# Staging the output gates by PSUM bank: from two shared tiles of 1024 columns to tiles of 512

## The chip, the cores and the metric

The kernel runs on one core of one Trainium2 chip. The metric is the device time of one execution in microseconds (us); lower is better. The kernel is written in Python with a tile framework. Its author gives the order of the program and the pools of buffers; a planner then lays out each engine's instruction stream by simulating the program with a cost table, taking what comes earlier in the program first where several instructions are ready. On the chip every engine works through its own stream in that order.

## What is computed

One layer of a trunk over 256 context tokens and 2048 latent tokens, 1024 wide:

```python
z = concat([hc, hx]) @ w_in                    # columns for four head groups
z_ml, z_rw, z_gl, z_gd = split(z)
mixed = concat([mlstm(z_ml), rwkv7(z_rw), gla(z_gl), gated_deltanet(z_gd)])
x = x + gate1 * (mixed[latent] @ w_out)
x = x + gate2 * (square(relu(rms(x) @ w1)) @ w2)
out = rms(x)
```

Each mixer runs a forward and a backward scan over 36 chunks of 64 tokens. The output of three of the mixers is multiplied by an **output gate**, a sigmoid or SiLU of columns of `z`: `sigmoid(o)` for mLSTM, `silu(og)` for GLA, `silu(zg)` for DeltaNet. The change concerns how these gates get from the product `z` to the place where the scans read them.

## The kernel before

**Stages.** The projection is computed in rounds over parts of the tokens. In each round the scans' inputs go to scratch tensors in HBM, and from there the scans take them chunk by chunk. After the fifth round comes a stage that the code calls the gap (L1889 and L1890): four calls of `out_gates`, each over 512 tokens, compute the output gates, and 16 scan steps (`group`) are interleaved with them, six forward (chunks 18 to 23) and ten backward (chunks 25 to 16). Then the tail follows: the output projection (`ps_o`), the MLP (`ps_f`, `ps_a`) and the last norm in four blocks of tokens, with the last 24 scan steps interleaved. The first tail block needs chunks 16 to 23 to be finished.

**An output gate tile.** `out_gates` (L1276) first builds the normed input `hh`, `hl` (`make_h`, L533: eight tiles `xh` of 512 columns are loaded, multiplied on GpSimd, scaled and copied on ScalarE and subtracted on VectorE; there is one `hh` and one `hl`, so the next `make_h` writes them when the last product has read them). Then it computes three gates through `gate_tiles` and `tm_tiles` (L861). `tm_pair` (L593) loads the weights, splits them in two parts (`w_hi`, `w_lo`) and multiplies: one PSUM bank `ps_z` takes 256 tokens by 256 columns, from 48 matmuls, and a tile of 512 tokens has two such banks. The pool `pd` has two banks in all. For each bank `fill` computes a tanh on ScalarE (into `gate`, a tile of the tag `b2`) and then, on VectorE, the gate itself into the staging tile, called `tm`. For a SiLU gate this last instruction reads the PSUM bank too. The staging tile is then stored to `x_gat` in HBM by `tm_out` (L636), which issues two DMAs per store on SyncE's queue (SP).

**Buffers.** The staging tile before is a `t4`: 1024 columns of the tag `x4`, of which there are two buffers (L1240). The tag `b2` has seven buffers of 512 columns (L1232). A buffer goes to its next tile when all readers and writers of the tile before it are done, a store's DMA included, and tiles take the buffers of a tag in the order of the program.

**Solves.** The RWKV and DeltaNet scans need triangular systems solved ahead of each pair of chunks (`solve`, L1287). A batch of up to four such units runs through three steps: `prep` per unit (loads, the products `ps_n`, a store to `x_sN`), one `find` for the batch (31 steps of two elementwise instructions, then a store to `x_sX`) and `post` per unit (loads, the products `ps_s` in two steps, a store to `x_t`). Each `prep`, `find` and `post` takes two tiles of 1024 columns. The batches queued in the fifth round (L1886) run beside each other: the first and third use the tags `s_b` and `s_x`, of one buffer each; the second, four units, uses **`x4`** for both tiles (L1847), the tag of the gates' staging tile. In the trace, which leaves buffer numbers out, the tiles on `x4` are called `s_x`, those on the other tags `s_s_b` and `s_s_x`.

**Order.** `interleave` takes one step of `out_gates` (one bank) at a time and then one entry of the solve queue. 24 steps remain of that queue when the gap begins: the last two `prep` of the second batch, the four `post` of the first, the second's `find`, the third's two `prep`, the second's four `post`, then the third's `find`, five empty entries, its two `post`, and three entries `ml_final`. So gate tiles and solve tiles alternate in the two buffers of `x4`. All of `ps_n`, `ps_s` and the scans' output products (`ps_ym`, `ps_ylgr`) share one PSUM buffer of the tag `yy`, in the order of the program.

Of the kernel before, what the change touches and what calls it, by code (L numbers as in the profile page):

```python
# [176 lines left out]
class Kern:  # L177
# [171 lines left out]
    def fill(self):  # L349

        X = self.X
        one = self.sp.tile([128, 1024], F32, tag="s_x", name="s_s_x", bufs=self.sb["s_x"])
        self.G.memset(one[:, :NCH], 1.0)
        for ft in range(2):
            c = 588 + 129 * ft
            for par, p in enumerate(SL):
                self.dma(X["tm"][:, :, par, c:c + 1].rearrange("c t o -> t c o"), one[p, :NCH].unsqueeze(2))
# [503 lines left out]
    def tm_tiles(self, i, chunks, dst, f0, fill, r=None):  # L861

        banks = self.tm_pair(i, r)
        st = self.t4("tm").rearrange("p (i r w) -> p i r w", r=2, w=128)
        for x, b in enumerate(banks):
            fill(st[:, 2 * x:2 * x + 2].rearrange("p i r w -> p i (r w)"), b)
            if x + 1 == len(banks) or chunks[x + 1] != chunks[x] + 4:
                a = next(j for j in range(x + 1) if chunks[x] - chunks[j] == 4 * (x - j))
                c0, n = chunks[a], 4 * (x + 1 - a)
                self.tm_out(st[:, 2 * a:2 * x + 2], dst[c0:c0 + n, :, :, f0:f0 + 128], n)  # L870
            yield
        if len(banks) == 1:
            yield
# [1054 lines left out]
```

## Time and profile before

| what | value |
| --- | --- |
| median of 3 runs | 4183.04 us (4180.95 to 4185.43) |
| the profiled execution | 4181.71 us |
| its span, from the first to the last instruction | 4179.9 us |
| mean granted TensorE clock | 0.875 |
| TensorE matmul busy | 3462.1 us (83%) |
| VectorE busy | 2490.3 us (60%) |
| ScalarE, GpSimd busy | 34%, 35% |

PE is TensorE's matmuls, PEld its weight loads, DVE is VectorE, ACT ScalarE, POOL GpSimd, SP SyncE, whose queue issues the DMAs. In rows of groups, a name such as `tm<-gate,ps_z` means that the instruction writes `tm` and reads `gate` and `ps_z`; `[4.76 <-DMA x_gat<-tm]` behind an instruction says that its engine sat idle for 4.76 us before it, and what ended that. Most elementwise instructions carry the line of a small helper (L185, L189, L193, L198), so tiles tell them apart.

### The profile page before, as it was taken

The numbers are of one execution on the slowest core, as the hardware profiler recorded it, in microseconds if no ns is written. First come the engines' busy times: TensorE is split into PE (matmuls) and PEld (weight loads), VectorE is DVE, ScalarE is ACT, GpSimd is POOL, SyncE is SP. The second block draws the span as 40 slices with busy tenths as digits, with TensorE's granted clock in tenths as the row PEclk, the third lists the DMA queues.
The fourth block names the chain that finished last, engine by engine and source line by source line (L and its number), as shares of the span: only waits on it lengthen the run. The fifth ranks groups of instructions, "written<-read, shape, count | busy, mean of one in ns | idle before, by whom it ended". The sixth has DMA issues, their size and how long they took to land.

```text
span 4179.9 us, 75082 instructions
## 1 busy us (share of the span) xinstructions
PE 3462.1 (83%) x29082; PEld 2807.3 (67%) x29082; DVE 2490.3 (60%) x5259; ACT 1403.3 (34%) x2544; POOL 1464.4 (35%) x1682
## 2 busy tenths in 40 slices
PE   6465877867777876658896999999999999999998
PEld 5344666656556765547785777777778777877786
DVE  6673866764776585536865556567754464445444
ACT  3334334434433433323332323233322332233222
POOL 3221834552626253502242333334322232223222
PEclk9667978877887876768898999999999999999999
DMA  5568478657686864647777444454532333232322
GB/s 205 108 180 149 116 157 194 143 131 146 153 150 160 187 144 124 171 121 193 212 212 195 124 135 148 138 171 142 175 95 96 106 102 115 96 98 91 104 96 86
DMA packets 610372, 592.66 MB, mean 142 GB/s; under 512 B 286384, under 2 KB 487168, under 8 KB 610016
## 3 DMA queue, kind: packets, MB, share of 16 engines
q1 hardware_dynamic: 610016, 587.87, 53.9%
q8 instruction: 229, 3.75, 0.4%
q14 instruction: 127, 1.04, 0.1%
HBM read 463.78 MB, written 123.92 MB: 141 GB/s over the span
## 4 chain that ended last, share of the span: by engine, by line
PE 42%; DVE 4%; issue 1%; POOL 1%; ACT 1%; DMA 1%; SPq 0%; POOLq 0%; DVEq 0%; ACTq 0%
PE ps_a L240 17%; PE ps_f L240 15%; PE ps_o L240 4%; PE ps_ylgr L229 1%; PE ps_z L212 1%; PE ps_S L229 1%; PE ps_att L240 1%; DVE h2l L193 1%; DVE relu L185 1%; PE ps_R L229 1%; SPq L201 0%; PE ps_ym L229 0%; PE ps_yT L248 0%; PE ps_ml L240 0%; POOL yall L185 0%
## 5 line engine op out<-in xcount | busy, mean ns | idle before, releaser
L185 POOL TENSOR_TENSOR w_lo<-w_f,w_hi 128x1024 fp32r<-128x1024 f32 x213 | 513.9, 2413 | 1232.8 <-ACT w_hi L198 1144.1
L198 ACT ACTIVATE w_hi<-w_f 128x1024 fp32r<-128x1024 f32 (+1 forms) x427 | 448.5, 1051 | 878.1 <-PE ps_a L240 387.1
L240 PE MATMUL ps_a<-ah,w_hi 128*128 128x512 f32 x1024 | 408.0, 403 | 8.0 <-ACT ah L198 8.0
L240 PE MATMUL ps_f<-h2l,w_hi 128*128 128x512 f32 x1024 | 402.8, 394 | 8.7 <-DVE h2l L193 8.7
L185 DVE TENSOR_TENSOR w_lo<-w_f,w_hi 128x1024 fp32r<-128x1024 f32 (+1 forms) x214 | 275.0, 1285 | 222.4 <-ACT w_hi L198 218.2
L240 PE MATMUL ps_f<-h2h,w_hi 128*128 128x512 f32 x1024 | 404.4, 395 | 3.5 <-ACT w_hi L198 2.7
L240 PE MATMUL ps_a<-al,w_hi 128*128 128x512 f32 x1024 | 406.2, 397 | 1.0 <-DVE al L185 1.0
L240 PE MATMUL ps_f<-h2h,w_lo 128*128 128x512 f32 x1024 | 405.5, 396 | 1.1 <-DVE w_lo L185 1.1
L240 PE MATMUL ps_a<-ah,w_lo 128*128 128x512 f32 x1024 | 399.9, 398 | 0.0
L240 PE MATMUL ps_z<-hh,w_hi 128*128 128x512 f32 (+3 forms) x760 | 301.7, 403 | 73.7 <-ACT hh L198 34.2
L193 DVE SCALAR_TENSOR_TENSOR x1T<-ps_a,modv,x1T 128x512 f32<-128x512 f32 x256 | 188.0, 749 | 259.6 <-PE ps_a L240 258.9
L240 PE MATMUL ps_z<-hh,w_lo 128*128 128x512 f32 (+3 forms) x760 | 299.4, 395 | 21.2 <-DVE w_lo L185 11.0
L240 PE MATMUL ps_z<-hl,w_hi 128*128 128x512 f32 (+3 forms) x760 | 298.3, 393 | 2.1 <-DVE hl L185 1.9
L185 DVE TENSOR_TENSOR relu<-relu 128x512 f32<-128x512 f32 x128 | 188.4, 1473 | 113.0 <-ACT relu L198 112.9
L212 PE MATMUL ps_z<-w_hi,hh 128*128 128x256 f32 x672 | 210.3, 315 | 36.0 <-ACT hh L198 21.9
L240 PEld LDWEIGHTS ps_a<-ah,w_hi 128*128 128x128 f32 x1024 | 191.2, 189 | 64.7 <-ACT ah L198 16.5
L240 PEld LDWEIGHTS ps_z<-hh,w_hi 128*128 128x128 f32 (+1 forms) x760 | 155.2, 206 | 111.5 <-ACT hh L198 37.5
L240 PEld LDWEIGHTS ps_f<-h2l,w_hi 128*128 128x128 f32 x1024 | 193.9, 189 | 51.7 <-DVE h2l L193 10.7
L240 PEld LDWEIGHTS ps_f<-h2h,w_hi 128*128 128x128 f32 x1024 | 194.0, 190 | 46.0 <-ACT w_hi L198 4.4
L240 PEld LDWEIGHTS ps_a<-ah,w_lo 128*128 128x128 f32 x1024 | 193.4, 189 | 45.5 <-issue 0.3
L240 PEld LDWEIGHTS ps_a<-al,w_hi 128*128 128x128 f32 x1024 | 193.6, 189 | 44.8 <-DVE al L185 1.2
L240 PEld LDWEIGHTS ps_f<-h2h,w_lo 128*128 128x128 f32 x1024 | 193.9, 189 | 43.5 <-DVE w_lo L185 1.9
(430 smaller groups left out, 7976.9 us busy)
## 6 DMA issues: line engine op xcount, KB each, us to landing
w_f<-w SPq DMA_DIRECT2D x256, 512.0 KB
w_f<-wg SPq DMA_DIRECT2D x90, 512.0 KB
tm<-x_tm SPq DMA_DIRECT2D x144, 259.5 KB
kc<-x_fm SPq DMA_DIRECT2D x64, 448.0 KB
adaw<-ada SPq DMA_DIRECT2D x48, 512.0 KB
rw<-x_rows SPq DMA_DIRECT2D x144, 160.0 KB
w_f<-wp SPq DMA_DIRECT2D x44, 512.0 KB
w_f<-wout SPq DMA_DIRECT2D x32, 512.0 KB
```

The source lines that it names most:

```text
L185: return (e or self.V).tensor_tensor(out=o, in0=a, in1=b, op=op)
L193: return self.V.scalar_tensor_tensor(o, a, s, b, op0, op1)
L198: return self.S.activation(o, a, f, bias=bias, scale=scale)
L212: i = self.T.matmul(o, l, r, start=k == 0, stop=k == len(mms) - 1)
L229: i = self.T.matmul(t.t[rows, cols], l, r, start=not prev, stop=not any(left[q] for q in quarters), skip_group_check=True)
L240: return self.T.matmul(o, l, r, start=start, stop=stop)
```

## The change

For the output gates (`r is None`) each bank now gets a staging tile of its own, a `t2` of 512 columns from the tag `b2`, and is stored as soon as it is filled, in a store of four chunks. The values, the matmuls, the fills and the number of steps that `interleave` sees stay the same. The tiles of `v_tiles`, where `r` is a round, keep the old way.

```diff
     def tm_tiles(self, i, chunks, dst, f0, fill, r=None):
         banks = self.tm_pair(i, r)
+        if r is None:
+            for c, b in zip(chunks, banks):
+                st = self.t2("tm")
+                fill(st.rearrange("p (i w) -> p i w", i=2), b)
+                self.tm_out(st.rearrange("p (i r w) -> p i r w", r=2, w=128), dst[c:c + 4, :, :, f0:f0 + 128], 4)
+                yield
+            if len(banks) == 1:
+                yield
+            return
         st = self.t4("tm").rearrange("p (i r w) -> p i r w", r=2, w=128)
         for x, b in enumerate(banks):
             fill(st[:, 2 * x:2 * x + 2].rearrange("p i r w -> p i (r w)"), b)
```

Before, a tile whose two banks cover neighbouring chunks was stored once, after its second fill, by two DMAs; the three tiles of the first `out_gates` call, whose banks lie apart, were stored twice, by four. Now all twelve tiles are stored in two stores of two DMAs each.

## The prediction

> **What bounds the kernel now.** I read the page first, then the windows around the gap, then the gate tiles and who waits for them, and last the chain of waits.
>
> ```profile
> PE   6465877867777876658896999999999999999998
> ...
> PEclk9667978877887876768898999999999999999999
> ```
>
> Each digit is a slice of 104.5 us. From slice 22 on TensorE is nearly full; before it there are two dips, slices 16 and 17 (1672 to 1881 us) and slice 21 (2194 to 2299 us). The gap lies there. Cut by stage, each row gives the stretch, its length, each engine's busy time and count, the granted clock, the DMA share and GB/s:
>
> ```profile
> core 0: us, PE busy (x) PEld busy (x) DVE busy (x) ACT busy (x) POOL busy (x), PEclk, DMA share, GB/s
> 1738.00:1773.00 35.00, 21.73 (x100) 17.91 (x100) 15.32 (x23) 15.69 (x24) 30.41 (x39) 0.61 0.63 161
> 1773.00:1898.00 125.00, 62.68 (x1191) 55.32 (x1190) 44.82 (x156) 29.40 (x82) 8.31 (x17) 0.64 0.51 124
> 1898.00:2212.00 314.00, 279.65 (x4463) 252.95 (x4464) 222.25 (x630) 121.64 (x252) 102.11 (x114) 0.90 0.75 207
> 2212.00:2286.00 74.00, 38.66 (x716) 31.35 (x716) 33.95 (x116) 12.51 (x29) 18.21 (x22) 0.82 0.67 188
> 2286.00:4179.00 1893.00, 1834.60 (x11298) 1458.57 (x11293) 1022.28 (x1574) 581.27 (x836) 579.99 (x372) 0.98 0.38 119
> ```
>
> In the stretch of 125 us no engine is half busy but TensorE, with 62.68 us. The next 314 us have TensorE busy for 89% (279.65 / 314), and the tail for 97% (1834.60 / 1893) at a granted clock of 0.98. So the tail is bound by TensorE and moves as a block: what the gap loses or gains ahead of it appears in the end one to one. The same windows for the gates' products alone:
>
> ```profile
> 1773.00:1898.00 125.00, 2.27 (x19) 2.07 (x18) 0.00 (x0) 0.60 (x1) 0.64 0.51 124
> 1898.00:2212.00 314.00, 155.91 (x1055) 140.74 (x1056) 10.04 (x15) 12.52 (x21) 0.90 0.75 207
> ```
>
> The 125 us hold next to none of the gates' products (19 matmuls of 1152), although TensorE has room; the crowded 314 us hold 1055. Why, the gate tiles say (durations min/median/max, first and last start):
>
> ```profile
> L198 ACT ACTIVATE gate<-ps_z x24: 578/597/598, 1772.3 to 2212.4; 128x512 f32<-128x512 f32 x24
> L193 DVE SCALAR_TENSOR_TENSOR tm<-gate,ps_z x16: 680/687/689, 1898.4 to 2213.7; 128x512 f32<-128x512 f32 x16
> ```
>
> The first bank's tanh starts at 1772.3, the fill that needs it only at 1898.4: 126.1 us in which both banks of `pd` are full and the third product can't start. VectorE's stream and its waits give the reason:
>
> ```profile
> 1897.76 0.42 DVE L185 TENSOR_TENSOR s_x<-s_x,ps_n 128x256 f32<-128x256 f32 x1
> ...
> 1898.43 1.28 DVE L193 SCALAR_TENSOR_TENSOR tm<-gate,ps_z 128x512 f32<-128x512 f32 x2
> ```
> ```profile
> DVE tm L193 <- DMA x_sN<-s_x: 3.2, 1, 3.2
> ```
>
> The fill runs right behind a `prep` of the batch on `x4`: the staging tile waits for buffers that these solves hold. It goes the other way too. These three rows of the timeline (GpSimd, SP, VectorE) show the second batch's `find`, whose memset waits for a gate tile's store:
>
> ```profile
> 1978.76 0.96 POOL L1302 MEMSET s_x<- 128x1024 f32 x1 [4.76 <-DMA x_gat<-tm]
> ```
> ```profile
> 1975.00 0.45 SPq L201 DMA_DIRECT2D x_gat<-tm  x1
> ```
> ```profile
> 1971.86 0.69 DVE L193 SCALAR_TENSOR_TENSOR tm<-gate,ps_z 128x512 f32<-128x512 f32 x1
> ```
>
> Late in the gap the gates' products stand in the way of the scans. In the chain of waits from 2082 to 2212 us:
>
> ```profile
> by line: PE ps_z L212 29.1%; PE ps_ylgr L229 8.0%; DVE hl L185 5.0%; PE ps_S L229 4.2%; issue 4.2%; PE ps_R L229 3.8%; PE ps_att L240 3.2%; DMA tm<-x_tm 2.8%; PE ps_ml L240 2.5%; SPq L201 2.4%; DVE s_s_x L185 2.3%; DMA s_s_b<-x_sX 2.2%; ACT
> ...
> 2111.70 3.07 PE ps_z L212 x24
> ```
>
> 29.1% of 130 us is 38 us of products that the scan steps wait behind, in bursts such as the one of 24 matmuls in 3.07 us.
>
> **The change part by part.**
>
> *The lock goes.* With staging on `b2`, gate tiles and solves share no buffer. The fill needs only its tanh, so the third product and those behind it can run from 1773. TensorE is idle there for 125.00 - 62.68 = 62.3 us. Not all of it can be used: a `make_h` falls in it, and products arrive in bursts. Bounds are 0 and 62.3; I take two thirds, 41.5 us. At 155.91 / 1055 = 148 ns a matmul that is 280 matmuls, about six banks. At the stretch's own clock of 0.64 a matmul would cost 148 x 0.90 / 0.64 = 208 ns and the same 41.5 us hold only 200 of them, worth 33 us later. I take 148, because more products in the stretch are what the 0.90 row has. The Trainium skill ("TensorE: Matmul & The Clock Gate", Part 1, "What's actually happening") says that the array is throttled by default and activity releases it; by that rule the 148 ns holds and the sum stands, without it the sum is some 13 us smaller. No run so far shows this stretch filled.
>
> *What it is worth later.* The 314 us stretch loses 41.5 us of TensorE work. At its own density of 0.89 it is 41.5 / 0.89 = **46.6 us** shorter. The bound above is 62.3 / 0.89 = 70; below it is 0, if the scans' own dependencies set the pace.
>
> *What becomes late: the solves of the first stretch.* Their products now share TensorE with the gates'. These are the last four `post` of the fourth round (two steps of 32 matmuls each) and eight `prep` (one step each), whose rows for 1773 to 1926 us are:
>
> ```profile
> L240 PE MATMUL ps_s<-s_s_b x128: 236/236/258, 1777.7 to 1821.5; 32*32 32x32 f32 x128
> L240 PE MATMUL ps_s<-s_s_x x128: 236/236/255, 1780.5 to 1823.4; 32*32 32x32 f32 x128
> ```
> ```profile
> L240 PE MATMUL ps_n<-s_s_b x128: 218/306/366, 1832.8 to 1870.0; 64*64 64x64 f32 x128
> L240 PE MATMUL ps_n<-s_x x128: 218/218/366, 1880.1 to 1920.1; 64*64 64x64 f32 x128
> ```
>
> 512 matmuls in 16 steps, one after another, since they share `yy`. Each step can wait from nothing to a whole burst: 16 x 3.07 = 49 us at most. I take a quarter, **12 us**: half of the steps meet a burst, halfway through. What is queued behind them on TensorE is the next product, gate or scan, and the scans of the gap start from their results.
>
> *make_h comes earlier.* It keeps its count:
>
> ```profile
> L185 POOL TENSOR_TENSOR xh<-xh,rbr x32: 1258/1272/2303, 1748.5 to 2140.6; 128x512 f32<-128x512 f32 x32
> L198 ACT ACTIVATE xh<-xh,modv,A x32: 797/812/817, 1749.7 to 2146.2; 128x512 f32<-128x512 f32 x32
> L198 ACT ACTIVATE hh<-xh x32: 612/630/632, 1750.6 to 2147.4; 128x512 fp32r<-128x512 f32 x32
> L185 DVE TENSOR_TENSOR hl<-xh,hh x32: 675/802/1798, 1751.3 to 2149.2; 128x512 fp32r<-128x512 f32 x32
> ```
>
> Eight `xh` cost ScalarE 8 x 1.44 = 11.5 us and GpSimd 10.2 us. In the first stretch these engines are busy for 29.40 and 8.31 us of 125, so this hides, at the price of a solve's ScalarE instruction now and then behind one of 0.8 us. Now 12 tiles of `b2`, not 6, lie between the `xh` of one call and the next, in seven buffers: the next call's fourth and sixth `xh` need buffers of its last two staging tiles. From the store's issue at 1975.00 to the memset that it released at 1978.76 is 3.8 us, what the first three `xh` take on GpSimd (3 x 1.27); cost nothing, or 3 x 3.8 = 11 us if all three later calls wait.
>
> *More stores.*
>
> ```profile
> L201 SPq DMA_DIRECT2D x_gat<-tm x30: 359/480/1743, 1899.6 to 2214.9; - x30
> ```
>
> 30 issues become 48 (24 banks x 2), of half the size in nine tiles of twelve. 18 x 0.480 = 8.6 us more on SP, spread over some 400 us. Behind them stand loads for solves and scans. I take 0; 8.6 us if every one delays the chain.
>
> The fills, the tanhs and 1152 matmuls are the same.
>
> *Sum*: 46.6 - 12 = 34.6 us less. 4181.71 - 34.6 = 4147.1 for the profiled execution; the median of before lies 1.3 us above it, so **4148.4**. The planner lays out the whole program after 1773 us anew; I allow 10 us for that in the range.
>
> **The rivals.**
>
> *A larger gain: the lock also paces the solves.* The second batch's `post`, on `x4`, go (within 1740 to 2260 us):
>
> ```profile
> L240 PE MATMUL ps_s<-s_x x192: 185/212/258, 2029.6 to 2090.6; 32*32 32x32 f32 x192
> ```
>
> Its four units start over 2029.6 to about 2090, 20 us apart, while the four of 1777.7 to 1821.5 are about 14 us apart: 3 x 6 = 18 us, and 4.8 us before `find`. If also the 38 us of products leave the scans' chain, because most gates are done by then, the gain is 18 + 4.8 + 38 + the 46.6 less 12 that I forecast, of which the 38 overlaps about half: some 76 us, **4107**. For it: the rows above. Against: the gap's TensorE work remains, and 89% busy leaves little room. Anything beyond 60 us I count here.
>
> *Slower: the first stretch's solves decide.* They pay the full 49 us, and the later stretch gains only the locks' 18 + 4.8, since the scans are paced by their own results: 49 - 23 = 26 us slower, **4209**. It decides from the point at which the 16 steps lose more on average than the later stretch gains: 46.6 / 16 = 2.9 us a step by my value. For it: these steps are serial, with one PSUM buffer, and a product ahead in the stream can't be overtaken. Against: a burst is 3.07 us, so nearly every step would have to meet a whole one.
>
> *No change: the scans pace the gap.* The gates move into the hole, but the scan steps follow one another by their states and by `yy`, and slice 21 only empties further: the first stretch's 12 us is paid and 12 to 20 us come back, **4179**. Against it speaks the 29.1% of `ps_z` in their chain.
>
> *Stores one behind another.* If each of the 18 further stores holds up the chain by its 3.8 us, 68 us are lost against 34.6 won: 4216. The Trainium skill ("DMA: Bandwidth & Descriptors", "Anatomy of one DMA — SWDGE (gpsimd) path") gives about 2.0 us of fixed cost for each DMA, mostly the write's receipt, on a path other than SP's; an estimate by it is 18 x 2.0 = 36 us, which would cancel the gain. Against it: nothing but the reuse of a buffer waits for a store, and `b2` has seven.
>
> **How the numbers follow.** Forecast (gain of 8.4 to 60 us) 0.55; larger gain 0.20; no change 0.10; slower by the solves 0.12, by the stores 0.03. About 0.2%, 8.4 us, is what a measurement of this kernel can tell from no change. Faster 0.75, same 0.10, slower 0.15. The range goes from 4083 (the larger gain with the bound of 70 for 46.6) to 4189 (no change, with the planner's 10): what is left out is slower by more than that, 0.12, and some 0.06 below.
>
> **What would show it.** Right: the first fill stands within 2 us of its tanh near 1772; the stretch 1773 to 1898 holds 200 or more of the gates' matmuls at a clock above 0.64; the wait of `find`'s memset for `x_gat<-tm` is gone; the last tanh comes well before 2212; the tail, cut at 2286 here, starts 25 to 50 us earlier and keeps its 1893 us. Wrong: `ps_s` and `ps_n` of the first stretch spread out by more than 30 us; or the last gates are early and the scans end as late as before; or the tail changes its length, which would mean that the planner's new order, not the lock, made the difference.

## The result, and the profile after

| | median of 11 runs | profiled execution | its span |
| --- | --- | --- | --- |
| before | 4179.62 us | 4181.71 us | 4179.9 us |
| after | 4199.22 us | 4194.23 us | 4192.4 us |

The ratio is 1.006 (95%: 1.0044 to 1.0075): the change costs about 20 us. The forecast was 34.6 us the other way. The two profiled executions lie 12.5 us apart, less than the medians; after's is the quickest of its runs.

The hole did close. These are the page's rows of TensorE and of its granted clock in 40 slices (of 104.8 us), after:

```profile
PE   6465877867777866696685999999999999999998
...
PEclk9667978877887876687886999999999999999999
```

Slice 17 (1782 to 1887 us) went from 5 to 9. But slices 18, 19 and 20 went from 8, 8, 9 to 6, 6, 8, and slice 21 from 6 to 5. The windows, at the cuts of before:

```profile
core 0: us, PE busy (x) PEld busy (x) DVE busy (x) ACT busy (x) POOL busy (x), PEclk, DMA share, GB/s
1773.00:1898.00 125.00, 109.30 (x1488) 100.28 (x1486) 54.65 (x124) 53.45 (x110) 31.59 (x26) 0.88 0.66 177
1898.00:2212.00 314.00, 227.42 (x3900) 201.80 (x3900) 201.31 (x612) 92.16 (x206) 72.19 (x90) 0.82 0.67 180
2212.00:2286.00 74.00, 39.55 (x702) 32.73 (x702) 29.89 (x111) 12.61 (x32) 23.24 (x33) 0.66 0.38 110
2286.00:4192.00 1906.00, 1840.02 (x11582) 1463.07 (x11582) 1042.80 (x1627) 586.85 (x850) 580.18 (x376) 0.99 0.39 122
```

The 125 us hold 109.30 us of matmuls where they held 62.68, but fewer instructions of VectorE (124 for 156): part of the other work in this stretch moved on. The next 314 us are 72% full (227.42 / 314), where they were 89% full. What is left behind 2286 us is 1906 us, 13 us more. The gates' products alone, in the same two cuts:

```profile
1773.00:1898.00 125.00, 75.84 (x512) 68.71 (x510) 5.48 (x8) 7.15 (x12) 0.88 0.66 177
1898.00:2212.00 314.00, 95.28 (x576) 82.97 (x576) 5.46 (x8) 7.14 (x12) 0.82 0.67 180
```

512 products stand in the first stretch instead of 19, at 75.84 / 512 = 148 ns each. TensorE's other work in it fell from 60.4 us (62.68 - 2.27) to 33.5 (109.30 - 75.84). The gate tiles:

```profile
L198 ACT ACTIVATE gate<-ps_z x24: 579/597/600, 1773.8 to 2184.5; 128x512 f32<-128x512 f32 x24
L193 DVE SCALAR_TENSOR_TENSOR tm<-gate,ps_z x16: 669/686/690, 1774.4 to 2187.2; 128x512 f32<-128x512 f32 x16
```

The first fill follows its tanh by 0.6 us, not 126.1, and the last tanh starts 28 us earlier. What pays for this is the solves of the first stretch:

```profile
L240 PE MATMUL ps_s<-s_s_b x160: 184/191/257, 1784.6 to 1968.0; 32*32 32x32 f32 x160
...
L240 PE MATMUL ps_n<-s_s_b x128: 218/218/366, 1859.8 to 1896.8; 64*64 64x64 f32 x128
L240 PE MATMUL ps_n<-s_x x128: 218/218/366, 1909.5 to 1964.7; 64*64 64x64 f32 x128
```

The last `prep` product of the stretch starts at 1964.7, before at 1920.1. From the first `ps_s` (1784.6, before 1777.7) the sixteen steps take 37.7 us longer. The timeline of TensorE and of ScalarE around the first of them:

```profile
1778.16 0.39 PE L212 MATMUL ps_z<-w_hi,hh 128*128 128x256 f32 x1 [0.86 <-DVE tm L193]
1778.95 0.38 PE L212 MATMUL ps_z<-w_lo,hh 128*128 128x256 f32 x1 [0.41 <-POOL w_lo L185]
...
1779.53 0.30 PE L212 MATMUL ps_z<-w_hi,hl 128*128 128x256 f32 x1
1779.65 0.39 PE L212 MATMUL ps_z<-w_hi,hh 128*128 128x256 f32 x1
1779.84 0.42 PE L212 MATMUL ps_z<-w_lo,hh 128*128 128x256 f32 x1
...
1782.83 0.40 PE L212 MATMUL ps_z<-w_hi,hh 128*128 128x256 f32 x1
1783.04 0.30 PE L212 MATMUL ps_z<-w_lo,hh 128*128 128x256 f32 x1
1783.18 0.28 PE L212 MATMUL ps_z<-w_hi,hl 128*128 128x256 f32 x1
...
1784.58 0.24 PE L240 MATMUL ps_s<-s_s_b 32*32 32x32 f32 x2
```
```profile
1779.14 1.72 ACT L198 ACTIVATE s_s_b<-s_s_b 32x256 f32<-32x256 f32 x4 [0.49 <-DMA s_s_b<-x_sX]
1785.84 0.76 ACT L198 ACTIVATE s_s_x<-ps_s 32x256 f32<-32x256 f32 x2 [4.98 <-issue]
```

ScalarE has the solve's whole input ready at 1780.86 (the last of four instructions ends at 1779.14 + 1.72). Its product starts at 1784.58: in between TensorE works off products of a gate bank that stand ahead of it in the stream. This one step waits 3.7 us.

For the experiments I cut each profile by its own events. **Stage 1** runs from the first gate's tanh to the first `ps_s` of the `post` of the fifth round's first batch (it holds the sixteen steps), **stage 2** from there to the start of the last of the gap's 16 scan steps (its first `ps_S`), **stage 3** to the first `ps_o`. From there it is the tail; "rest" is stage 3 and the tail together. All in us:

| | stage 1 | stage 2 | stage 3 | rest |
| --- | --- | --- | --- | --- |
| before | 155.3 | 301.9 | 32.8 | 1950.4 |
| after | 193.4 | 275.6 | 48.4 | 1949.6 |

So 38 us are lost in stage 1 and 26 are won in stage 2; these 12 us are the difference of the two profiles. Of the 38, 5.4 lie ahead of the first `ps_s`, 20.1 in the four `post` and 12.6 in the eight `prep`. In the single records of the trace the eight products of the `post` start 16.4 us in sum after the last copy of their input, in before 2.0 (each taken at the third of its 32 matmuls, as the first two need the first copy alone): so 14 of the first 25 us are waits in TensorE's stream. The rest varies by some 10 us between single profiles of like kernels.

### The profile page after: what moved, and what is told of

Read it like the earlier page. It is cut to its first block, busy times and chain, and to the rows that moved or that the text cites. A ratio compares the mean times of both kernels' runs of the same rounds, so it can differ in the third digit from the quotient of the medians.

```text
span 4192.4 us, 75080 instructions
## 1 busy us (share of the span) xinstructions
PE 3458.4 (82%) x29082; PEld 2804.4 (67%) x29082; DVE 2497.2 (60%) x5259; ACT 1403.1 (33%) x2544; POOL 1462.6 (35%) x1682
## 5 line engine op out<-in xcount | busy, mean ns | idle before, releaser
L240 PEld LDWEIGHTS ps_f<-h2h,w_hi 128*128 128x128 f32 x1024 | 193.4, 189 | 45.0 <-ACT w_hi L198 4.4
```

The lines of the kernel that those rows point to most:

```text
L240: return self.T.matmul(o, l, r, start=start, stop=stop)
```

## The experiments

The runs were made on several chips, on which the kernel before takes from 4146.76 to 4179.62 us; each ratio is against the kernel before on the same chip, and lengths of stages of runs on different chips compare only roughly. Five theories stood against each other. **Q**, the queue: the solves' products stand in TensorE's stream behind products of gates which now come early, and pass the delay on. **The `b2` rival**: staging in `b2` holds up the `xh` of the next `out_gates` call. **S**, the stores: the additional ones hold up loads on SP. **E**, the other engines: the early gates' work holds up the solves on ScalarE, VectorE, SP or DMA, and not in TensorE's order. **L**, the layout: the planner's new order of everything behind, whatever the change is.

### Who makes stage 1 longer: the lock's end, the buffers or the stores

*e1_split* keeps the staging tile on `x4`, and stores by the bank as the change does:

```diff
-            if x + 1 == len(banks) or chunks[x + 1] != chunks[x] + 4:
-                a = next(j for j in range(x + 1) if chunks[x] - chunks[j] == 4 * (x - j))
+            if r is None or x + 1 == len(banks) or chunks[x + 1] != chunks[x] + 4:
+                a = x if r is None else next(j for j in range(x + 1) if chunks[x] - chunks[j] == 4 * (x - j))
```

> Staging stays on x4 in one tile of 1024 columns, as before; only the store is split by bank (48 issues for 30). Theory Q (the solves' products queue on TensorE behind the gates' products, which now come early): nothing comes early here, so within 8 us of before, 4172 to 4188. Rival S (the 18 further stores cost the time): 4190 to 4205, as the changed kernel.

*e2_hold* is the changed kernel with the first product of the gates' third bank ordered on TensorE behind the last `prep` product of the second batch: staging in `b2`, gates late.

```diff
+HOLD = {2: 59}
...
+            if after and k == 0:
+                self.tc.add_manual_dep(i.ins, after, ORDER, ...)
```

> The changed kernel with staging on b2, but the gates' third bank is ordered on TensorE behind the last prep of the second batch, so the solves of the hole have TensorE to themselves again. Theory Q: the loss goes; the first post of the queue's first batch starts its ps_s near 1928 as before, not 1967, and the time is 4165 to 4185. Rival B (staging on b2 itself is slow, because make_h's loads wait for it) and rival S: still 4190 to 4205.

*e3_paced* lets the banks go early, but each of banks 2 to 12 behind the product of one solve, in turn, by the same means (`HOLD = {2: 48, 3: 49, 4: 50, ...}`).

> The changed kernel, with each early gate bank ordered on TensorE right behind one solve's product (banks 2 to 5 behind the four post, 6 to 11 behind prep, one or two steps on, 12 behind the first post of the next batch): a bank then runs while the solve is on VectorE and its DMAs. Theory Q: the solves keep their pace (first ps_s of the next batch at 1928 to 1945), ten banks are still early, and the time is 4140 to 4175, below both kernels. Rival E (early gates hurt through ScalarE, VectorE, SP or DMA, not through TensorE's order): the first ps_s comes at 1955 or later and the time is 4185 to 4205.

*e4_a5* is the changed kernel with the staging tile in another tag than `b2`:

```diff
-                st = self.t2("tm")
+                st = self.pp.tile([128, 512], F32, tag="a5", name="tm", bufs=4)
```

> The changed kernel with the staging tiles on the tag a5 (four buffers of 512 columns, shared with the scans' yp) and not on b2, so that make_h's xh no longer wait for stores. Theory Q: as the changed kernel, 4190 to 4210. Rival B: make_h's eight xh go back from 24 us to some 14 and 10 us or more come back, 4175 to 4190.

| | stage 1 | stage 2 | stage 3 | ratio (95%) |
| --- | --- | --- | --- | --- |
| after | 193.4 | 275.6 | 48.4 | 1.006 (1.0044 to 1.0075) |
| e1_split | 156.0 | 332.5 | 33.3 | 1.0094 (1.0079 to 1.011) |
| e2_hold | 156.7 | 336.4 | 33.6 | 1.0098 (1.0072 to 1.0125) |
| e3_paced | 179.0 | 276.2 | 46.1 | 1.0039 (1.0024 to 1.0054) |
| e4_a5 | 192.2 | 276.7 | 44.8 | 1.0069 (1.0052 to 1.0085) |

That early gates make stage 1 longer is shown: with the gates late, by the lock (e1) or by an order without it (e2), it is back at 156. With other buffers it stays at 192. With the banks rationed it is 179: an order on TensorE alone takes back 14 of the 38 us, and the waits of the `post` in its stream fall from 16.4 to 4.2. But Q, taken as the only cause, had the first `ps_s` of the next batch at 1928 to 1945 and a time below both kernels; it came at 1947.9, and the ratio is 1.0039. So Q has a part of the loss, and E is not excluded for the rest. The wait which I had priced at 11 us for the buffers of `xh` did appear, in GpSimd's waits for loads of `xh` from 1900 to 2260 us. First after, then e4:

```profile
POOL xh L185 <- DMA xh<-xT: 27.3, 6, 9.4
```
```profile
POOL xh L185 <- DMA xh<-xT: 23.9, 6, 9.5
```

It is nearly as long in e4, where no staging tile lies in `b2`, and the time is the same. So `b2` is not its cause, and that rival falls.

What I had not expected is that e1 and e2, forecast at 4165 to 4188 us, are slower than after: their stage 2 is 31 to 35 us longer than that of before, though its gates come as late as there.

### How much a mere new layout does

Four kernels differ from before or after by nothing but an order. n1 and n3 compute the three gates in another order, n2 and n4 issue the two DMAs of a gate's store the other way round:

```diff
-        for i, silu, c in ((6, True, 256), (20, False, 0), (26, True, 128)):
+        for i, silu, c in ((20, False, 0), (6, True, 256), (26, True, 128)):
```

> The kernel before with the three gates of each out_gates call in another order (20, 6, 26 for 6, 20, 26): the same instructions, buffers and stores, but the planner lays the streams out anew from the gap on. Theory L (the difference between the two kernels is mostly which layout the planner hits): this moves the time by 8 us or more, most likely up, to 4175 to 4215. Rival (early gates, theory Q, or the split stores, theory S, are what costs): within 8 us of before.

> The kernel before with the two DMAs of each gate store issued in the other order: again no work is changed. Theory L: 8 us or more from before, most likely slower. Rivals Q and S: within 8 us of before.

> The changed kernel with the gates in the order 20, 6, 26. Theory L: anywhere from 4165 to 4215, its first post of the queue's first batch late as in the changed kernel (ps_s at 1955 or later), since that part is theory Q and not the layout; what the later stretch gives back varies by 10 us or more. Rivals Q and S alone: within 8 us of the changed kernel.

> The changed kernel with the two DMAs of each gate store in the other order. Theory L: as for the run with the other order of gates, 4165 to 4215, 8 us or more from the changed kernel. Rivals Q and S alone: within 8 us of the changed kernel.

| | stage 1 | stage 2 | stage 3 | ratio (95%) |
| --- | --- | --- | --- | --- |
| n1, before, other order | 164.6 | 327.9 | 38.7 | 1.0094 (1.0063 to 1.0126) |
| n2, before, swapped | 154.1 | 300.3 | 35.2 | 1.0006 (0.9993 to 1.0019) |
| n3, after, other order | 192.8 | 275.0 | 45.8 | 1.0065 (1.0043 to 1.0086) |
| n4, after, swapped | 190.8 | 274.9 | 45.8 | 1.0052 (1.0035 to 1.0068) |

(The first gate of n1 is another one; from its first `post` on its stage 1 is 153.9, before 150.0.) After is robust: three layouts give 1.005 to 1.0065, with a stage 2 of 275 us in each. Before is not: one order of the gates has 26 us more in stage 2, as e1 and e2 have. So what the change costs hangs on the layout that it is compared with. In the swapped order it loses as well (n4 4189.38 us, n2 4173.31). In the other order of the gates it loses nothing: n3 takes 4196.01 us and n1 4207.77 on the same chip, with intervals that overlap; there stage 1 pays 28 us from its first `post` on, and stage 2 wins 53.

One wait grows in the slow layouts, that of VectorE's `ga` for its chunk's load from 1900 to 2260 us. The rows of before, e1, n1 and after (total, times, longest):

```profile
DVE ga L185 <- DMA tm<-x_tm: 1.8, 3, 1.0
```
```profile
DVE ga L185 <- DMA tm<-x_tm: 12.7, 6, 3.8
```
```profile
DVE ga L185 <- DMA tm<-x_tm: 10.7, 6, 4.3
```
```profile
DVE ga L185 <- DMA tm<-x_tm: 18.2, 10, 8.0
```

n2, at 300.3, has 1.8 too, e2 17.1. But after has 18.2 with a stage 2 of 275.6, so this wait doesn't set the length of the stage, and the cause of the 26 to 35 us isn't found. And the additional stores are no explanation: n1 has 30 and is slow, e13 below has 48 and a stage 2 of 300.4.

### Does TensorE's load set the pace of stage 2

e5 (before) and e6 (after) compute only one of the three products that make up an output gate's `z`, 16 matmuls a bank for 48:

```diff
-                    mms += [(hh, wh), (hh, wl), (hl, wh)]
+                    mms += [(hh, wh), (hh, wl), (hl, wh)] if r is not None else [(hh, wh)]
```

> The kernel before, with the output gates computed from the first of their three products alone (w_hi times hh: 16 matmuls a bank for 48). Its run is the base for the next one. Stage 1 (first tanh of a gate to the first ps_s of the post of the fifth round's first batch) stays at 155 us, since no gates run there; stage 2 (from there to the last scan step's ps_S) falls from 302 to 250 to 280 us, by less products and by the layout; time 4120 to 4165.

> The changed kernel with the same third of the gates' products. Theory Q (solves' products queue on TensorE behind the gates'): the 37 us by which stage 1 grew shrink to about a third, stage 1 at 160 to 175 us, and the time comes to within 12 us of the thinned kernel before. Rival E (early gates hurt through make_h, weights, SP and DMA, which are all still there): stage 1 at 180 to 193 us and the time 20 us or more above it.

| | stage 1 | stage 2 | stage 3 | ratio (95%) |
| --- | --- | --- | --- | --- |
| e5, before, a third | 161.9 | 288.8 | 46.0 | 1.0013 (1.0001 to 1.0025) |
| e6, after, a third | 179.9 | 262.4 | 46.0 | 0.9996 (0.9984 to 1.0007) |

This is the run that meets the forecast's main term. The windows of stage 2, of before and of e5:

```profile
1927.60:2229.50 301.90, 263.24 (x4425) 236.24 (x4425) 213.15 (x604) 119.83 (x249) 105.36 (x116) 0.91 0.73 202
```
```profile
1918.40:2207.20 288.80, 205.20 (x3736) 177.79 (x3739) 204.87 (x585) 110.35 (x236) 92.87 (x107) 0.76 0.75 205
```

TensorE is relieved of 58 us (263.24 - 205.20), and the stage is 13 us shorter. At a density of 0.87 (263.24 / 301.90) it would be 67. TensorE thins out to 71% instead (205.20 / 288.80), and the clock goes from 0.91 to 0.76. Both the stage (250 to 280) and the time (4120 to 4165) came out longer than I had expected. The program as a whole gains nothing, although two thirds of 1152 matmuls are gone: stage 3 grows by the same 13 us. So the stage was full of TensorE work and not bound by it. A neutral order moves stage 2 by up to 26 us, so one pair alone would be weak; after and e6 give the same 13 us (275.6 - 262.4). In stage 1 the change costs 18 us with a third of the products (179.9 against 161.9) and 38 with all of them: the delay shrinks with the products, as Q has it, but less than in proportion (a third would be 13), and 179.9 lies outside the 160 to 175 of Q, at the edge of E's 180 to 193. E has a share here: the eight products of the `post` wait only 2.5 us in TensorE's stream in e6 (2.0 in e5), though the `post` take 67.4 us for 52.2. The timeline of ScalarE at the third of them, of e6 and of e5:

```profile
1802.32 0.81 ACT L198 ACTIVATE xh<-xh,modv,A 128x512 f32<-128x512 f32 x1 [0.20 <-POOL xh L185]
1803.04 1.70 ACT L198 ACTIVATE s_s_b<-s_s_b 32x256 f32<-32x256 f32 x4
```
```profile
1790.02 1.72 ACT L198 ACTIVATE s_s_b<-s_s_b 32x256 f32<-32x256 f32 x4 [1.27 <-DMA s_s_b<-x_sX]
```

In e5 ScalarE, idle, copies the solve's input 1.1 us after the issue of its load ended. In e6 it is on `make_h` of the next call and copies 6.5 us after it. Whether the load was late as well, the rows don't tell.

### Only four banks early, and is the rest make_h

e7 lets four banks in beside the four `post`, one behind each, and holds the next one until the last `prep` of the second batch (`HOLD = {2: 48, 3: 49, 4: 50, 5: 51, 6: 59}`):

> The changed kernel with banks 2 to 5, those of the first out_gates call, ordered behind the four post of the fourth round, one each, and all later banks held until the last prep of the fifth round's second batch: early banks without a make_h between them. Theory Q: stage 1 at 155 to 163 us; stage 2 between the two kernels, 285 to 300; with a stage 3 of 35 to 48 the time is 4160 to 4185. Theory L adds up to 30 us to stage 2, as in the other layouts. Rival E: stage 1 at 170 or more.

Stage 1 is 168.9, stage 2 279.0, stage 3 46.6; the ratio is 1.0002 (0.9985 to 1.002). Four of the ten or so early banks have nearly all of the gain in stage 2 and a little over a third of the loss in stage 1, which lies between Q's 155 to 163 and E's 170. The products of the `post` wait only 3.5 us in TensorE's stream here, for 2.0 in before, though the `post` take 7 us longer; 3 of these are the load for the fourth, which ScalarE, idle, awaits until 4.2 us after its issue ended (1.2 in before); e2, with its gates late, has that delay too (4.5). Of what is left, `make_h` was a suspect: the next call's `hh` is built in this stage. e9 was to hold it behind the same `prep`:

```diff
+                if late and k == 0:
+                    self.tc.add_manual_dep(i.ins, late, ORDER, ...)
```

> As the run with banks 2 to 5 released one by one and the rest held, but the next out_gates call's make_h is held as well (its first ScalarE instruction is ordered behind the third-last product copy of the second batch's prep on ScalarE). If make_h among the solves costs the remaining 13 us of stage 1, stage 1 falls from 169 to 155 to 160 us and the time to 4155 to 4170; if the four early banks themselves cost it, stage 1 stays at 165 to 170.

Stage 1 167.7, stage 2 289.6, ratio 1.0037 (1.0025 to 1.0048). This run didn't do what it was meant to: only the first of eight `xh` was held, the other seven were scaled and copied as early as in e7. e13 holds all eight (`if late:`).

> The paced kernel with make_h's first ScalarE instruction of all eight k, not of one, held behind a ScalarE copy of the first stretch's last solves; the gates that need hh follow it. The before has stage 1 at 155, the paced one at 169. If what is left of stage 1 is make_h's pacing of the products that the solves stand behind, stage 1 is 155 to 160 and stage 2 near 285, the ratio at 1.003 or less; if it is not make_h but the four banks let in among the post, stage 1 stays at 165 to 170 and the ratio near the paced one's 1.000 to 1.004.

Stage 1 170.3, stage 2 300.4, ratio 1.0045 (1.0028 to 1.0061). Here the copies to `hh` do come late, as the rows of stage 1 show, and the gates' products in the stretches of the four `post` and of the eight `prep`:

```profile
L199 ACT ACTIVATE hh<-xh x7: 615/617/632, 1909.6 to 1914.7; 128x512 fp32r<-128x512 f32 x7
```
```profile
1751.50:1815.00 63.50, 32.65 (x192) 30.45 (x192) 0.69 (x2) 2.39 (x4) 0.76 0.55 132
1815.00:1915.90 100.90, 5.66 (x30) 5.51 (x30) 0.67 (x1) 0.00 (x0) 0.66 0.66 173
```

So what is left in e7 isn't `make_h`, which stands among the `prep` there; in after it stands among the `post`, which this run doesn't test. The `post` take 63.5 us, 8.4 more than in before (1777.7 to 1832.8), beside 192 products of gates, four banks. The `prep` take 6 us more than before (100.9 for 94.8) beside 30 products; e5, a kernel with its gates late, takes 101.0 for them too, so these 6 us may be layout; the cause stays open.

### What the early gates run into: the finishing's one buffer

After each of the last scan steps a chunk is finished (norms, gates, a transpose `ps_yT`) in a tile `yall`, of which there is one. In after, VectorE's first instruction for the next chunk waits for the transpose of the chunk ahead (timeline):

```profile
2235.58 0.29 DVE L185 TENSOR_TENSOR yall<-ps_ym,dn 128x128 f32<-128x128 f32 x1 [2.14 <-PE ps_yT L248]
...
2248.10 0.29 DVE L185 TENSOR_TENSOR yall<-ps_ym,dn 128x128 f32<-128x128 f32 x1 [1.67 <-PE ps_yT L248]
...
2260.51 0.29 DVE L185 TENSOR_TENSOR yall<-ps_ym,dn 128x128 f32<-128x128 f32 x1 [2.64 <-PE ps_yT L248]
```

They come 12.5 us apart, and the transpose of the last of the eight chunks that the first `ps_o` needs starts 28.8 us after the last scan step's start, before 15.3. e8 gives these tiles four buffers of another tag:

```diff
+            if second and "gat" not in self.lb:
+                yall = self.pp.tile([128, 512], F32, tag="a5", name="yall", bufs=4)
```

> The changed kernel with the scans' output tile yall of second visits on a tag of four buffers (a5) in place of its one buffer. Stage 3 (last ps_S to the first ps_o) went from 33 to 48 us; the theory is that the scan steps now end faster than the finishing of their outputs, one each 12.3 us through one yall. If so, stage 3 falls to 40 us or less and the time by 5 to 15 us, to 4183 to 4195. If it is another thing (the tail's loads), stage 3 stays at 45 to 48.

The 28.8 us become 16.4, and 1.006 becomes 1.0032 (1.0018 to 1.0046); the two intervals overlap at their ends. Stage 3, expected at 40 us or less, shrinks only from 48.4 to 42.9, and stage 2 is 7 us longer (283.0). Then the same in the other orders:

> Banks 2 to 5 released one by one, the rest held, and yall of second visits on the tag of four buffers. If stage 3 is the finishing through one yall, stage 3 falls from 47 to 35 to 43 us, and the time to 4155 to 4170, below before (4170); theory L adds or takes up to 15 us in stage 2.

> Both: make_h held and yall on four buffers. If both terms are real and add, stage 1 is 155 to 160, stage 2 275 to 285, stage 3 35 to 43 and the time 4145 to 4162, faster than both kernels.

> The kernel before with yall of second visits on the tag of four buffers. There the scan steps end no faster than their outputs are finished, so stage 3 stays at 31 to 35 us; by theory L stage 2 lies anywhere from 300 to 335, and the time at 4165 to 4210.

> The same with the last finishing's tile on a tag of four buffers. If the finishing's buffer costs here what it cost in the paced kernel, 25 us off the run before (which was 0.9942 for the paced one with it): ratio 0.990 to 0.997. If stage 2 grows by what stage 1 loses, as it did with one k held, it is at 1.000 or above, and the paced one with four buffers stays the best.

| | without (ratio) | with four buffers (ratio, 95%) | rest, without | rest, with |
| --- | --- | --- | --- | --- |
| before | 1 | e12: 0.9992 (0.9979 to 1.0006) | 1950.4 | 1948.9 |
| after | 1.006 | e8: 1.0032 (1.0018 to 1.0046) | 1949.6 | 1938.8 |
| four banks early (e7) | 1.0002 | **e10: 0.9942 (0.9921 to 0.9963)** | 1961.5 | 1933.1 |
| e9, one `xh` held | 1.0037 | e11: 1.0026 (1.0009 to 1.0044) | 1957.8 | 1936.0 |
| e13, eight `xh` held | 1.0045 | e14: 0.9998 (0.9987 to 1.001) | 1943.8 | 1934.9 |

In the kernel before, the buffer is worth nothing. With gates early it is worth 0.3 to 0.6%, but for e9, where 0.1% is within the intervals. The columns "rest" are single profiles; in the first three rows the two columns come from different chips.

The buffers do a second thing, which I hadn't foreseen. In all five kernels that have them, two of the last 24 scan steps start before the first `ps_o`, in the other fifteen none. So stage 3 does not get short (41.9 us in e10, 41.3 in e11), and in e12 and e14 it grows to 40 (32.8 in before, 32.7 in e13), while the tail has less to do: 11242 products in e10's last row below, 11582 in that of after. How much of the gain comes from the transposes and how much from these two steps isn't shown. With them go two misses: e11, forecast to beat both kernels, has 165.2 us in stage 1 and 307.9 in stage 2, and e14 gains 17 us on e13 (4166.76 to 4149.64), where 25 were forecast.

e10 beats both kernels, 4123.47 us against 4146.76 of before on its chip. Its windows, cut at its own stages 1, 2 and 3 and the tail:

```profile
1743.00:1914.00 171.00, 104.91 (x1618) 95.06 (x1617) 79.91 (x232) 51.08 (x120) 25.23 (x31) 0.71 0.61 157
1914.00:2188.00 274.00, 245.70 (x4332) 219.55 (x4331) 198.57 (x587) 103.59 (x225) 92.60 (x107) 0.92 0.73 204
2188.00:2230.00 42.00, 27.77 (x485) 22.59 (x481) 24.75 (x91) 7.72 (x20) 13.44 (x21) 0.67 0.87 236
2230.00:4121.00 1891.00, 1829.26 (x11242) 1454.20 (x11240) 1026.44 (x1565) 579.98 (x834) 572.69 (x367) 0.99 0.37 120
```

Against before, stage 1 pays 15 us and stage 2 wins 28 with TensorE at 90% (245.70 / 274). That is some 12 of the 24 us that the ratio stands for; the others lie behind the last scan step of the gap, and no run separates them.

## Why the prediction was wrong

**Right: what the change does.** The lock went, and the first stretch filled. The 148 ns for a product was right too: the stretch's clock rose from 0.64 to 0.88, and the rule of the Trainium skill ("TensorE: Matmul & The Clock Gate", Part 1) that activity releases the clock holds here. The number of products was too small: I let 280 move, 493 did (512 - 19), 73.6 us of TensorE's time for 41.5. That is above the bound of 62.3, which took the idle time of before for all the room that there is; another 27 us of TensorE's other work left the stretch.

**Failed first: what becomes late.** "I take a quarter, 12 us" measured 38. The bound of 49 stood in the text; the value was taken from a burst as seen in the crowded stretch, and for a solve that meets one in every second step. In after six of the eight products of the `post` wait 1.7 to 4.2 us each in TensorE's stream, 14 us more in sum than in before. `make_h`, put at nothing because "this hides", isn't cleared: it stands ahead of a solve's copies on ScalarE in e6, and how much of the 38 us is its own isn't shown. In all it is 38 / 16 = 2.4 us a step. By the runs the loss grows with the banks let in: 13.6 us for the four of e7 (3.4 each), 23.7 for the eleven of e3 (2.2 each), 38 for the 493 / 48 = 10 or so of after (3.8 each), a third to a half of the 7.1 us (48 x 148 ns) that a bank takes on TensorE. The order e2, which takes the banks out of this stretch and leaves all else of the change, takes stage 1's loss back, though not the program's: its stage 2 is one of the long ones (336.4 us).

**Failed second: what it is worth later.** "At its own density of 0.89" was wrong as a step, not only in its size. 89% busy was read as bound by TensorE. With what really moved, this rule gives 73.6 / 0.89 = 83 us; stage 2 won 26, and e5 and e6 show that the rule doesn't hold: 58 us less on TensorE are worth 13. The condition of the bound below, "if the scans' own dependencies set the pace", fits these runs better than the rule does; which dependency it is wasn't found. The gain doesn't go with the number of products that move: e7, with four banks early, has 23. Nor is 26 a fixed worth of the change: against the other layout of before (n1 and n3) stage 2 wins 53, and the forecast of 46.6 would have looked right there by luck.

**Not foreseen: the next wait.** The text asked what is late next for the solves, not for the end of the scans, where one `yall` paces the finishing at 12.5 us a chunk. e8 puts the buffer at 0.0028 of 4180 us, 12 us, with intervals that overlap at their ends, and with the two scan steps of the tail in it.

**The rivals.** "Slower" came nearest: 49 - 23 = 26 us slower, measured 20. Its first half was right, the solves' share, 38 for 49. Its second was not: the 23 were to come from the lock on the second batch's `post` and `find`, and those `post` got no quicker (below), so that 23 is near the 26 by luck. The two profiles differ by 38 - 26 = 12 us, the medians by 20; no stage is shown for the other 8. Its argument against, that nearly every step would have to meet a whole burst, was no argument: the stretch had room for bursts because it was empty. "Larger gain" fell with its ground, the lock as the pace of the second batch's `post`. In after they share `x4` with no gate, and still go 21 us apart (the four start at 2069.6, 2086.4, 2109.9 and 2133.8; before 20):

```profile
L240 PE MATMUL ps_s<-s_x x192: 191/191/258, 2069.6 to 2134.3; 32*32 32x32 f32 x192
```

The stores cost nothing that these runs can see: e13 with 48 has the stage 2 of before with 30. The estimate of 36 us by the Trainium skill ("DMA: Bandwidth & Descriptors", "Anatomy of one DMA — SWDGE (gpsimd) path") is not borne out for these.

**The signs.** Of those named for "right", the fill, the products, the clock and the last tanh came true; that the tail starts earlier didn't (first `ps_o` at 2291.2, before 2262.4). From there the tail did not keep its length either, a sign named for "wrong": 1901.2 us, before 1917.6, which makes up for the 15.6 us that stage 3 grew. The wait of `find`'s memset for a gate's store, which was to vanish, still stands there; GpSimd and SP, timeline:

```profile
1971.00 0.96 POOL L1312 MEMSET s_x<- 128x1024 f32 x1 [18.42 <-DMA x_gat<-tm]
```
```profile
1967.21 1.27 SPq L201 DMA_DIRECT2D x_sN<-s_x  x2
1968.52 1.87 SPq L201 DMA_DIRECT2D x_gat<-tm  x3
```

No gate tile lies on `x4` now. The memset comes 3.8 us after the issue of the last `prep`'s store, which it does need. The releaser that a row names is inferred, and here it can't be right; such a row alone couldn't show the lock in before either. The first sign for "wrong", a spread of `ps_s` and `ps_n` by over 30 us, came true at 37.7, and so did the second: the last gates are early, and the gap's last scan step starts 13 us later than before (2242.8 for 2229.5).

**Open**: how the 24 us of stage 1 that aren't waits of the `post` in TensorE's stream split between TensorE, ScalarE and the loads; the 6 us of the `prep` in e7 and e13; and what makes one layout of before 26 us longer in stage 2 than another.

## What to carry to other kernels

A stretch in which an engine idles beside a chain of small serial steps isn't free: on an in-order stream, what is put there stands ahead of the chain, and here a third to a half of its time became delay; rationing it, one bank beside each of four steps, kept most of the gain for a little over a third of the loss. A stage that is 89% full of an engine's work is bound by it only if less work makes it shorter: try that with a thinner product before dividing by the density. When a stage is made faster, look for the single buffer at its end, which cost nothing as long as the stage was slow. And where a planner lays out the streams, compare with a second layout of the kernel before: here a mere order of the gates moved it by 0.9%, more than the change.

## What the runs showed of the hardware

In after's timeline above, TensorE's products slow down for 3.2 us soon after two gaps of 0.86 and 0.41 us: from 1779.84 to 1783.04 they start 0.21 us apart and show 0.41 us each, before and after it 0.12 us apart and 0.28. These slow products made the burst that the solve waited for about 1.4 us longer (15 products by 0.09 us). The Trainium skill ("TensorE: Matmul & The Clock Gate", Part 1, "What's actually happening") has the halved clock come after an idle window of about 3.4 us; here no gap of that length stands ahead of it: the two short ones are all the idle time of TensorE in the 5 us before. That they brought it on isn't shown.

Taking work from TensorE also made the rest of its work dearer. The gates' products in stage 2, of before and of e5:

```profile
1927.60:2229.50 301.90, 134.65 (x905) 120.49 (x905) 9.45 (x14) 11.90 (x20) 0.91 0.73 202
```
```profile
1918.40:2207.20 288.80, 52.07 (x288) 43.77 (x288) 9.21 (x14) 10.66 (x18) 0.76 0.75 205
```

82.6 us of them went, but TensorE's sum fell by 58 only: the other products took 128.6 us for 3520 in before (37 ns each) and 153.1 for 3448 in e5 (44 ns), 1.2 times as long, as the clocks stand (0.91 / 0.76 = 1.2).
